# Storing all partitions of the attention's output bank, and adding its two parts where the branches load them

## The chip, the cores and the metric

One core of a Trainium2 chip runs the whole kernel. The metric is the device time of one execution in microseconds (us), as the median of several runs. The engines are TensorE (PE, with its weight loads PEld), VectorE (DVE), ScalarE (ACT), GpSimd (POOL) and SyncE (SP), which issues nearly all DMAs.

## The reference

One layer of an encoder on x of 1 x 1024 x 1024, all in float32 (`bias`, `window` and `sink` stand for longer code):

```python
h = rms_norm(x, norm_mix)
q_a, k_a, v_a, q_b, k_b, v_b, g_a, g_b = split(h @ w_in)      # 8 heads of 64; q_b 8 heads, k_b/v_b 2
o_a = softmax(q_a k_a / 8 + bias_a, window of 8 x 16 on the 16 x 64 token grid) v_a
o_b = softmax(q_b k_b / 8 + bias_b, sink, blocks within +-128 tokens) v_b
y = sigmoid(g_a) * (o_a @ w_branch_a) + sigmoid(g_b) * (o_b @ w_branch_b)
x = x + y @ w_out
h = rms_norm(x, norm_ffn)
x = x + (silu(h @ w_gate) * (h @ w_up)) @ w_down               # hidden width 2816
```

q and k are normalised per head as well.

## The kernel before

**Arithmetic.** TensorE multiplies reduced float32 (fp32r). A float32 operand is therefore split into a high part, which ACT writes by a copy, and a low part, which DVE writes by a subtract (`split`, L48 to L55; the two show up as L50 and L51). A product of two such operands takes three matmuls: high by high, high by low, low by high.

**Order of the work.** The instructions of PE stand in the order of the program. Those of DVE, ACT, POOL and SP are ordered by a scheduler, save where `tc.issue_after(x)` says that an instruction may only stand after x on its engine. A DMA on SP waits until the one issued eight before it is done.

**Attention (60 to 405 us in the trace).** The heads come in six groups, na0, sw0, na1, sw1, na2 and na3: groups of two neighbourhood heads and of four sliding-window heads, 16 heads in all. For each head and query block PE makes scores (L592, L593), and DVE, ACT and POOL turn them into probabilities `E` (L598 to L606). `flip` transposes them on PE (L616) and splits them into `ph` and `pl` (ACT, then DVE). `values` multiplies both by the values (L654). The stationary operand of that product holds the high part of v in columns 0 to 63 and the low part in columns 64 to 127, so the bank `o` collects the products with the high part in partitions 0 to 63 and those with the low part in 64 to 127. A head has two halves of 512 tokens, and there is one bank `o` (L39): the next half's first product waits until `store_half` has emptied it. Between the steps of the heads PE works through a list of other products: the projections of later groups, and the first gates (`pg`, L427 to L429).

**Emptying the bank.** `store_half` (L624 to L640) copies the half of the partitions that is not the head's own into the tile `of` (ACT, L636, 64 x 512) and adds the head's own half to it (DVE, L637, 64 x 512). Two heads of a pair fill 64 partitions each of one `of`, and after the second a DMA of 512 KB takes it to `o_dram` (L640), eight in all. `of` has one buffer.

**Gates.** Eight pairs of gates, d = 0 to 7. Those of d = 0 and 1 are plain products in the attention (their results `graw`, L454, go to `g_dram`); from d = 2 on `gate_pair` computes two by two blocks by seven products instead of eight (class `Seven`), p = 1 to 7, into four banks X, Y, V and Z. After some products a bank is copied to another by ACT (L836) to go on accumulating, and DVE reads the banks into `go` (L882 to L901). Gates 2 and 3 run product by product in turn and are marked `early`; their second operands, the row sums `ta`, `tb`, `hs` (L502 to L515), are made by DVE and ACT meanwhile, those of j = 0 and 1 still in the attention, each step of them after the instruction that `att["bound"]` names (L478): the last row maximum (L598). The weights of a gate come as `ga` and `gb`.

**Branches.** A row r of `o` is 128 features by 1024 tokens: rows 0 to 3 the neighbourhood heads, 4 to 7 the sliding-window heads. `load_o` (L924 to L928) loads four rows of one half, 256 KB each, and splits each. It is called four times: rows 4 to 7, half 0, after gate 5; rows 0 to 3, half 0, behind p = 6 of gate 7; rows 4 to 7, half 1, behind p = 2; rows 0 to 3, half 1, behind p = 3, with the two loads of the first sigmoid inputs (`load_sg(0, 0)`) ahead of it. Then 16 turns follow, each with two sigmoids on ACT (L993) and two products of twelve matmuls, first over rows 4 to 7, then over rows 0 to 3 (`pb`, L427 to L429); the second half is first used in the third turn.

Output projection and feed-forward follow, by the same seven products.

Of the kernel before, what the change touches and what calls it, by code (L numbers as in the profile page):

```python
# [19 lines left out]
HD = 64  # L20
# [5 lines left out]
def block_kernel(ctx, tc, x, xt, small, w_in, rpb, t5, w_ba, w_bb, w_out, w_gate, w_up, w_down,  # L26
# [18 lines left out]
    def f(ap):  # L45
        return ap.bitcast(F32)
# [40 lines left out]
    def half_cols(h):  # L87
        return slice(h * 512, h * 512 + 512)
# [6 lines left out]
    def dma(dst, src):  # L95

        tc.keep_in_program_order(nc.sync.dma_start(dst, src))
# [4 lines left out]
    def tok(t):  # L102
        return slice(t * P, (t + 1) * P)
# [68 lines left out]
    load_small()  # L172
    load_x(0, 0, 0)

    o_dram = drp.tile([8 * P, T], F32, name="o_dram")
    swe = drp.tile([8, 512], F32, name="swe")
    nae = drp.tile([64, 744], F32, name="nae")
    g_dram = drp.tile([32 * P, 512], F32, name="g_dram")
# [253 lines left out]
    def run(gen):  # L432
        for _ in gen:
            pass
# [94 lines left out]
    with tc.tile_pool(name="at", bufs=1) as ap:  # L529
# [48 lines left out]
        for gi, (kind, idx) in enumerate(order):  # L578
            nq, nk = (2, 2) if kind == "na" else (4, 1)
            heads += [dict(gi=gi, kind=kind, hl=hl, kl=hl * nk // nq, h=idx * nq + hl, nq=nq, O={}, E={}, P={})  # L580
                      for hl in range(nq)]
        of_tiles = {}

        def scores(hd, qb):
            q, k1, k2, v = groups[hd["gi"]]
# [23 lines left out]
        def flip(hd, kb):  # L609
            q0, q1 = max(0, kb - 1), min(7, kb + 1)  # L610
            n = (q1 - q0 + 1) * P
            nm_ = f"{hd['gi']}_{hd['hl']}_{kb}"
            tp = bank("t", "tp" + nm_)
            for j, qq in enumerate(range(q0, q1 + 1)):
                ko = (kb - max(0, qq - 1)) * P
                nc.tensor.transpose(tp[:, tok(j)], hd["E"][qq][:, ko:ko + P], ident)  # L616
            ph = ap.tile([P, 384], F32R, tag="ph", name="ph" + nm_, bufs=4)
            pl = ap.tile([P, 384], F32R, tag="pl", name="pl" + nm_, bufs=4)
            split(*(z[:, :n].rearrange("p (j i) -> p j i", i=P) for z in (ph, pl)),
                  tp[:, :n].rearrange("p (j i) -> p j i", i=P)[:, :, ::-1])  # L620
            hd["P"][kb] = (ph, pl)

        def store_half(hd, half):
            gi, e = hd["gi"], hd["hl"] % 2  # L624
            pair = (gi, hd["hl"] // 2)
            if pair not in of_tiles:
                of_tiles[pair] = ap.tile([P, T], F32, tag="of", name=f"of{gi}_{hd['hl']}", bufs=1)
            of = of_tiles[pair]
            own, oth = slice(e * HD, e * HD + HD), slice(HD - e * HD, 2 * HD - e * HD)
            O = hd["O"][half]  # L630
            if hd["kind"] == "na":
                dst, sh = of[own, half_cols(half)], lambda z: z
            else:
                dst = of[own, :].rearrange("p (s r c) -> p r s c", r=16, s=8)[:, 8 * half:8 * half + 8]
                sh = lambda z: z.rearrange("p (r s c) -> p r s c", r=8, s=8)
            nc.scalar.copy(dst, sh(O[oth, :]))  # L636
            nc.vector.tensor_add(dst, sh(O[own, :]), dst)  # L637
            if e == 1 and half == 1:
                row = ((0 if hd["kind"] == "na" else 4) + hd["h"] // 2) * P
                nc.sync.dma_start(o_dram[row:row + P, :], of)  # L640

        def values(hd, block):

# [152 lines left out]
    class Seven:  # L796
# [27 lines left out]
        def step(self, p, rows=None):  # L824

            hi, lo = self.prepare(p)
            z = {1: "X", 2: "X", 5: "V", 6: "Z" if self.early else "Y", 3: "Y"}.get(p, "Z")
            ps = self.banks[z]
            for j in range(self.n) if rows is None else rows:
                bh, bl = self.mv[p][j]  # L830
                first, end = j == 0 and (p in (1, 5) or self.early and p == 3), j == self.n - 1
                nc.tensor.matmul(ps, hi[:, tok(j)], bh, start=first, stop=False, skip_group_check=True)  # L832
                nc.tensor.matmul(ps, hi[:, tok(j)], bl, start=False, stop=False, skip_group_check=True)  # L833
                nc.tensor.matmul(ps, lo[:, tok(j)], bh, start=False, stop=end, skip_group_check=True)  # L834
            if p == 1 or p == 6 and not self.early:
                nc.scalar.copy(self.banks["Z" if self.early or p == 6 else "Y"], ps)  # L836

    class TokenSums(dict):

# [84 lines left out]
    def load_o(r0, half):  # L924
        for r in range(r0, r0 + 4):
            o_rows[r, half] = hi, lo = operand("H", f"o{r}_{half}")
            dma(f(lo), o_dram[tok(r), half_cols(half)])
            split(hi, lo, f(lo))  # L928


    wb, sgs = {}, {}
# [31 lines left out]
        load_branch(1)  # L963
        load_o(4, 1)

    def behind_three():
        load_sg(0, 0)
        load_o(0, 1)

    run(gate_pair(7, ORDER, {6: lambda: load_o(0, 0), 2: behind_two, 3: behind_three}))  # L970

    sets = bank_sets()
    my = {}
# [2 lines left out]
    def out_loads(i):  # L976
# [3 lines left out]
                w_out[0, :, tok(2 * i + a)].rearrange("(k p) c -> p k c", p=P))  # L980
        return Seven(f"o{i}", [two(z) for z in st], 4, my, sets)

    turns = [(2 * j + e, half) for j in range(4) for half in range(2) for e in range(2)]
    y = {}
    for n, (d, half) in enumerate(turns):
        j, c = d // 2, half_cols(half)
        if half == 0:
            y[d] = scratch2(f"y{d}")
        if n + 1 < len(turns):
            load_sg(*turns[n + 1])  # L990
        for br in (1, 0):
            sg = sgs[d, half, br]
            nc.scalar.activation(sg, sg, AF.Sigmoid)  # L993
        for br in (1, 0):
            pb = bank(RING[(2 * n + 1 - br) % 8], f"pb{d}_{br}_{half}")
            sg = sgs[d, half, br]
            run(product(pb, wb[d, br], [o_rows[4 * br + r, half] for r in range(4)]))
            if br:
                nc.vector.tensor_mul(y[d][:, c], pb, sg)
            else:  # L1000
                nc.vector.tensor_mul(sg, pb, sg)
                nc.vector.tensor_add(y[d][:, c], y[d][:, c], sg)
        if half == 0:
            p = 2 if d % 2 else 1
            my[p][j] = operand("U" if p == 1 else "V", f"y{p}_{j}")
            split(*my[p][j], y[d][:, c])
            if j < 3:
                load_branch(d + 2)
            elif d == 7:
                my[7], my[3] = ([operand("H", f"y{p}_{i}") for i in range(4)] for p in (7, 3))  # L1010
                for m, q in enumerate((7, 3)):
                    for i in range(3):
                        hi, lo = my[q][i]
                        row = (3 * m + i) * P
                        dma(f(lo), y_dram[row:row + P, :])
                        split(hi, lo, f(lo))
        elif d % 2:
            (b11, b12), (b21, b22) = halves(y[d - 1]), halves(y[d])
            t = TokenSums(f"y{j}", b11, b12, b22).rest(b21)
            for p in (5, 6):  # L1020
                my[p][j] = operand("U" if p == 5 else "V", f"y{p}_{j}")
                split(*my[p][j], t[p][0])
            for m, p in enumerate((7, 3, 4)):
                row = (3 * m + j) * P
                if j < 3:
                    dma(y_dram[row:row + P, :], t[p][0])
        if n == len(turns) - 2:
            pairs = {i: out_loads(i) for i in range(2)}
# [490 lines left out]
```

## Time and profile before

| | |
|---|---|
| median of 3 runs | 1326.53 us (1325.66 to 1327.61) |
| the profiled execution | 1324.66 us, its span 1322.9 us |
| PE busy in the span | 1306.8 us (99%) |
| DVE, ACT | 1037.3 us (78%), 699.3 us (53%) |
| granted clock of PE | 1.00 |

The profile shows one execution. A row of the timeline gives start, duration, engine, line and operation, what is written and read, the shape, and in brackets how long the engine stood idle before it and what released it. Rows of waits give the total, the number and the longest. Rows by stretch give the busy time of PE, PEld, DVE, ACT and POOL with the number of instructions, then PE's granted clock, the share of the DMA engines and GB/s. The buffers of a tile share a name in the trace: `o<-o_dram` are the loads of all rows.

### The profile page before, as it was taken

What the parts mean: (1) busy time and instruction counts of PE and PEld (TensorE: products, weight loads), DVE (VectorE), ACT (ScalarE), POOL (GpSimd) and SP (SyncE); (2) the same over time, 40 slices, a digit from 0 to 9 for tenths busy, and PEclk for the clock granted to TensorE, in tenths of its full rate; (3) what the DMA queues carried; (4) which work ended last, traced back from release to release, by engine and by line L of the source; (5) the groups of instructions that cost most, each with busy time, mean ns of one, the idle gap of its engine ahead of it and who ended that gap; (6) DMA issues with size and microseconds to landing.
All of it is one profiled execution on the core that took longest, in us unless ns stands there. A gap on an engine that the chain in (4) does not pass through costs nothing.

```text
span 1322.9 us, 19555 instructions
## 1 busy us (share of the span) xinstructions
PE 1306.8 (99%) x6618; PEld 1133.3 (86%) x6618; DVE 1037.3 (78%) x2069; ACT 699.3 (53%) x1459; POOL 172.4 (13%) x308
## 2 busy tenths in 40 slices
PE   9999999999999999999999999999999999999998
PEld 8999999999878788888887888888888888888887
DVE  5678878887787756778899887887777789798764
ACT  6667857786663334536457544434444456363532
POOL 1364645454220000000000000000000000000000
PEclk9999999999999999999999999999999999999999
DMA  9531313141424345748684532333333346672532
GB/s 311 145 88 40 92 51 94 45 118 51 130 88 167 116 138 166 250 145 259 203 290 120 159 112 80 98 118 100 92 112 119 121 167 215 239 255 64 178 129 83
DMA packets 177284, 183.52 MB, mean 139 GB/s; under 512 B 20464, under 2 KB 125936, under 8 KB 177184
## 3 DMA queue, kind: packets, MB, share of 16 engines
q1 hardware_dynamic: 176928, 182.18, 43.8%
q8 instruction: 52, 0.85, 0.3%
q14 instruction: 48, 0.39, 0.1%
q10 hardware_dynamic: 256, 0.10, 0.0%
HBM read 129.00 MB, written 48.18 MB: 134 GB/s over the span
## 4 chain that ended last, share of the span: by engine, by line
PE 84%; DVE 6%; DMA 4%; ACT 3%; issue 2%; POOL 1%; SPq 0%; ACTq 0%; DVEq 0%; POOLq 0%
PE bankZ L832 5%; PE bankZ L833 5%; PE bankZ L834 5%; PE bankY L833 5%; PE bankY L832 5%; PE bankY L834 5%; PE bankX L832 4%; PE bankX L834 4%; PE bankX L833 4%; PE pj L327 4%; PE pj L325 4%; PE pj L326 4%; PE bankV L833 3%; PE bankV L832 3%; PE bankV L834 3%; PE o L654 3%
## 5 line engine op out<-in xcount | busy, mean ns | idle before, releaser
L604 ACT ACTIVATE E<-E,nm 128x384 f32<-128x384 f32 (+3 forms) x128 | 75.7, 591 | 48.7 <-DVE nm L598 42.9
L606 POOL TENSOR_SCALAR E<-E,nm 128x384 f32<-128x384 f32 (+1 forms) x128 | 78.9, 617 | 103.8 <-DVE nm L605 72.3
L51 DVE TENSOR_TENSOR pl<-tp,ph 128x384 fp32r<-128x384 f32 (+1 forms) x128 | 66.3, 518 | 10.6 <-ACT ph L50 9.4
L50 ACT CAST ph<-tp 128x384 fp32r<-128x384 f32 (+1 forms) x128 | 57.4, 448 | 20.7 <-PE tp L616 19.6
L50 ACT CAST f<-f 128x512 fp32r<-128x512 f32 x87 | 51.3, 619 | 27.4 <-DMA f<-u_dram 22.4
L51 DVE TENSOR_TENSOR f<-f 128x512 fp32r<-128x512 f32 x87 | 56.5, 686 | 8.8 <-ACT f L50 8.7
L616 PE MATMUL tp<-ident,E 128*128 128x128 f32 x352 | 59.6, 273 | 0.1
L654 PE MATMUL o<-pl,v 128*128 128x256 f32 (+2 forms) x160 | 49.2, 308 | 4.0 <-DVE pl L51 3.9
L616 PEld LDWEIGHTS tp<-ident,E 128*128 128x128 f32 x352 | 45.2, 140 | 5.2 <-POOL E L606 0.3
L345 POOL TENSOR_TENSOR ss<-ss,mhalf 128x4 f32<-128x4 f32 (+2 forms) x42 | 49.1, 1170 | 3.1
L654 PE MATMUL o<-ph,v 128*128 128x256 f32 (+2 forms) x160 | 46.2, 303 | 3.2 <-DVE of L637 3.2
L592 PE MATMUL s<-k,q 128*128 128x384 f32 (+1 forms) x128 | 46.4, 363 | 0.0
L1213 POOL TENSOR_TENSOR rs<-rs,mhalf 128x4 f32<-128x4 f32 x2 | 2.9, 1444 | 321.5 <-DVE rs L1212 321.5
L593 PE MATMUL s<-k,q 128*128 128x384 f32 (+1 forms) x128 | 41.3, 323 | 0.0
L598 DVE CUSTOM_DVE_ANT_0 E<-s,bsw,cols 128x384 f32<-128x384 f32 (+1 forms) x64 | 36.8, 576 | 2.7 <-PE s L593 2.0
L1230 ACT ACTIVATE u<-u 128x512 f32<-128x512 f32 x44 | 27.7, 630 | 19.8 <-DVE u L1229 19.8
L598 DVE CUSTOM_DVE_ANT_0 E<-s,bna 128x384 f32<-128x384 f32 (+1 forms) x64 | 33.1, 517 | 4.8 <-PE s L593 4.2
L605 DVE RECIPROCAL nm<-nm 128x1 f32<-128x1 f32 x128 | 20.2, 159 | 21.1 <-ACT E L604 19.7
L1231 DVE TENSOR_TENSOR u<-u,wide_rs 128x512 f32<-128x512 f32 x44 | 30.2, 689 | 7.4 <-ACT u L1230 6.6
L654 PEld LDWEIGHTS o<-pl,v 128*128 128x128 f32 x160 | 30.1, 188 | 6.8 <-DVE pl L51 6.1
L833 PE MATMUL bankV<-f,f_5h 128*128 128x512 f32 x88 | 34.5, 392 | 1.0 <-DVE f L54 1.0
L654 PEld LDWEIGHTS o<-ph,v 128*128 128x128 f32 x160 | 30.1, 188 | 6.1 <-DVE of L637 5.3
(1266 smaller groups left out, 4650.7 us busy)
## 6 DMA issues: line engine op xcount, KB each, us to landing
f<-u_dram SPq DMA_DIRECT2D x77, 256.0 KB
wg_s<-in_w_gate_dram SPq DMA_DIRECT2D x22, 512.0 KB
u_dram<-u SPq DMA_DIRECT2D x33, 256.0 KB
sg<-g_dram SPq DMA_DIRECT2D x32, 256.0 KB
g_dram<-go SPq DMA_DIRECT2D x24, 256.0 KB
u_dram<-tau SPq DMA_DIRECT2D x22, 256.0 KB
u_dram<-tbu SPq DMA_DIRECT2D x22, 256.0 KB
rows<-in_x_dram SPq DMA_DIRECT2D x8, 512.0 KB
```

Source lines behind the costliest of these rows:

```text
L50: a = nc.scalar.copy(hi, src)
L51: b = (eng or nc.vector).tensor_tensor(lo, src, f(hi), ALU.subtract)
L325: nc.tensor.matmul(ps[:, :384], lh, his[k][:, :384], start=(k == 0), stop=False)
L326: nc.tensor.matmul(ps[:, :384], lh, los[k][:, :384], start=False, stop=False)
L598: att["bound"] = nc.vector.tensor_tensor_reduce(E[:, :n], s[:, :n], hd["bias"](qb), -1.0, sk if sw else 1e30, ALU.add, ALU.min, nm[:, 0:1] ...
L604: nc.scalar.activation(E[:, :m], E[:, :m], AF.Exp, bias=nm[:, 0:1], scale=-1.0, accum_out=nm[:, 1:2])
L606: nc.gpsimd.tensor_scalar(E[:, :n], E[:, :n], nm[:, 1:2], 1.0, op0=ALU.mult, op1=ALU.mult)
L616: nc.tensor.transpose(tp[:, tok(j)], hd["E"][qq][:, ko:ko + P], ident)
L654: nc.tensor.matmul(hd["O"][half][:, (a - half * 4) * P:(z + 1 - half * 4) * P], v[:, kb].rearrange("p a e -> p (a e)"), pp[:, (a - q0) * P ...
L832: nc.tensor.matmul(ps, hi[:, tok(j)], bh, start=first, stop=False, skip_group_check=True)
L833: nc.tensor.matmul(ps, hi[:, tok(j)], bl, start=False, stop=False, skip_group_check=True)
L834: nc.tensor.matmul(ps, lo[:, tok(j)], bh, start=False, stop=end, skip_group_check=True)
```

## The change

The copy out of the bank now takes all 128 partitions, and the add leaves the attention. `of` belongs to one head and still has one buffer; each head is stored by a DMA of its own, 16 of 512 KB, into an `o_dram` of twice the size. `load_o` loads two tiles per row, the products with the high parts (of two heads) and those with the low parts, 256 KB each, into the buffers where the split's results will stand, adds them on DVE into a scratch tile `os` of two buffers, and splits that. So 32 adds of 64 x 512 go, 16 adds of 128 x 512 come, and 16 loads and 8 stores more.

With it go three edits of the order: `att["bound"]` is also set by the subtract that writes `pl`; `load_sg(0, 0)` is called behind p = 1 of gate 7, with the branches' sigmoids held back until the copy of that gate's p = 6 (`last_copy`); and `Seven.step` keeps that copy.

```diff
-    o_dram = drp.tile([8 * P, T], F32, name="o_dram")
+    o_dram = drp.tile([16 * P, T], F32, name="o_dram")
...
-            split(*(z[:, :n].rearrange("p (j i) -> p j i", i=P) for z in (ph, pl)),
-                  tp[:, :n].rearrange("p (j i) -> p j i", i=P)[:, :, ::-1])
+            _, att["bound"] = split(*(z[:, :n].rearrange("p (j i) -> p j i", i=P) for z in (ph, pl)),
+                                    tp[:, :n].rearrange("p (j i) -> p j i", i=P)[:, :, ::-1])
...
         def store_half(hd, half):
-            gi, e = hd["gi"], hd["hl"] % 2
-            pair = (gi, hd["hl"] // 2)
-            if pair not in of_tiles:
-                of_tiles[pair] = ap.tile([P, T], F32, tag="of", name=f"of{gi}_{hd['hl']}", bufs=1)
-            of = of_tiles[pair]
-            own, oth = slice(e * HD, e * HD + HD), slice(HD - e * HD, 2 * HD - e * HD)
-            O = hd["O"][half]
+            if not half:
+                hd["of"] = ap.tile([P, T], F32, tag="of", name=f"of{hd['gi']}_{hd['hl']}", bufs=1)
+            of, O = hd["of"], hd["O"][half]
             if hd["kind"] == "na":
-                dst, sh = of[own, half_cols(half)], lambda z: z
+                nc.scalar.copy(of[:, half_cols(half)], O)
             else:
-                dst = of[own, :].rearrange("p (s r c) -> p r s c", r=16, s=8)[:, 8 * half:8 * half + 8]
-                sh = lambda z: z.rearrange("p (r s c) -> p r s c", r=8, s=8)
-            nc.scalar.copy(dst, sh(O[oth, :]))
-            nc.vector.tensor_add(dst, sh(O[own, :]), dst)
-            if e == 1 and half == 1:
-                row = ((0 if hd["kind"] == "na" else 4) + hd["h"] // 2) * P
-                nc.sync.dma_start(o_dram[row:row + P, :], of)
+                nc.scalar.copy(of.rearrange("p (s r c) -> p r s c", r=16, s=8)[:, 8 * half:8 * half + 8],
+                               O.rearrange("p (r s c) -> p r s c", r=8, s=8))
+            if half:
+                nc.sync.dma_start(o_dram[tok((0 if hd["kind"] == "na" else 8) + hd["h"]), :], of)
...
-                nc.scalar.copy(self.banks["Z" if self.early or p == 6 else "Y"], ps)
+                self.copied = nc.scalar.copy(self.banks["Z" if self.early or p == 6 else "Y"], ps).ins
...
     def load_o(r0, half):
         for r in range(r0, r0 + 4):
             o_rows[r, half] = hi, lo = operand("H", f"o{r}_{half}")
-            dma(f(lo), o_dram[tok(r), half_cols(half)])
-            split(hi, lo, f(lo))
+            for z, row in ((hi, 0), (lo, HD)):
+                src = o_dram[2 * r * P + row:2 * r * P + row + 1, half_cols(half)]
+                dma(f(z), bass.AP(src.tensor, src.offset, [[P * T, 2], [T, HD], [1, 512]]))
+            both = scratch(f"os{r}_{half}")
+            nc.vector.tensor_tensor(both, f(hi), f(lo), ALU.add)
+            split(hi, lo, both)
...
-    def behind_three():
-        load_sg(0, 0)
-        load_o(0, 1)
-
-    run(gate_pair(7, ORDER, {6: lambda: load_o(0, 0), 2: behind_two, 3: behind_three}))
+    run(gate_pair(7, ORDER, {1: lambda: load_sg(0, 0), 6: lambda: load_o(0, 0), 2: behind_two, 3: lambda: load_o(0, 1)}))
...
+    last_copy = pairs[7].copied
...
-            nc.scalar.activation(sg, sg, AF.Sigmoid)
+            with tc.issue_after(last_copy):
+                nc.scalar.activation(sg, sg, AF.Sigmoid)
```

The order of PE's instructions is the same in both kernels; lines below L623 have moved up by seven in the new one (L836 is L829 there). The order of three places has changed on the other engines.

On DVE at the last attention head (`pl_1_5` to `pl_1_7` are its last low halves, `of` with `o_1_0` is the head's first half), before:

```order
L515 SCALAR_TENSOR_TENSOR tb_5461<-xo_5379,cols,ta_5460 128x512
L51 TENSOR_TENSOR hs_1_5523<-tb_5461,hs_1_5523 128x512
L51 TENSOR_TENSOR hs_1_5499<-ta_5460,hs_1_5499 128x512
L51 TENSOR_TENSOR pl_1_5_5471<-tp_1_5_5466,ph_1_5_5470 128x384
L637 TENSOR_TENSOR of_0_5260<-o_1_0_5402,of_0_5260 64x512
L51 TENSOR_TENSOR hs_1_5535<-tb_5461,hs_1_5535 128x512
L51 TENSOR_TENSOR pl_1_6_5493<-tp_1_6_5488,ph_1_6_5492 128x384
```

And now:

```order
L454 TENSOR_TENSOR graw_0_0_5438<-pg_0_0_5309,wide_rs_110 128x512
L503 TENSOR_TENSOR ta_5445<-xe_5363 128x512
L51 TENSOR_TENSOR pl_1_5_5456<-tp_1_5_5451,ph_1_5_5455 128x384
L507 SCALAR_TENSOR_TENSOR ta_5445<-ta_5445,cols,g22h 128x512
L54 SCALAR_TENSOR_TENSOR hs_1_5462<-ta_5445,cols,hs_1_5462 128x512
L51 TENSOR_TENSOR pl_1_6_5478<-tp_1_6_5473,ph_1_6_5477 128x384
L511 SCALAR_TENSOR_TENSOR tb_5446<-xe_5363,cols,g22h 128x512
```

The add has gone, and the row sums of j = 1 stand behind the `pl` that stood behind them.

On DVE at the last product of gates 2 and 3 (`go_0_5707` and `go_0_5691` are gate 2's result in the two kernels, `s1g`, `s2g` and `g_5l` belong to the weights of gate 4), before:

```order
L51 TENSOR_TENSOR hs_3_5704<-tb_5689,hs_3_5704 128x512
L814 TENSOR_TENSOR s1g_5812<-gb_5809 128x512
L894 TENSOR_TENSOR go_0_5707<-bankZ_5553,gp_5709 128x512
L895 TENSOR_TENSOR go_0_5707<-bankY_5551,go_0_5707 128x512
L51 TENSOR_TENSOR g_5l<-s1g_5812,g_5h 128x512
```

And now:

```order
L51 TENSOR_TENSOR g_1l<-ga4s,g_1h 128x512
L807 TENSOR_TENSOR s1g_5796<-gb_5793 128x512
L51 TENSOR_TENSOR g_5l<-s1g_5796,g_5h 128x512
L807 TENSOR_TENSOR s2g_5797<-ga4s,s1g_5796 128x512
L887 TENSOR_TENSOR go_0_5691<-bankZ_5537,gp_5693 128x512
```

Two more rows of gate 4's weights stand ahead of the read of bank Z.

On ACT behind gate 5, where the first rows of `o` are split while gate 6 runs (with the numbers, since rows 4 to 7 read alike without them), before:

```order
L836 COPY bankY0_5551<-bankX0_5550 128x512
L50 CAST o4_0_6237<-o4_0_6237 128x512
L50 CAST o5_0_6241<-o5_0_6241 128x512
L50 CAST o6_0_6245<-o6_0_6245 128x512
L892 COPY gp6_6255<-bankV0_5552 128x512
L50 CAST o7_0_6249<-o7_0_6249 128x512
L836 COPY bankZ0_5553<-bankY0_5551 128x512
```

And now:

```order
L829 COPY bankY0_5535<-bankX0_5534 128x512
L50 CAST o4_0_6221<-os4_0_6224 128x512
L885 COPY gp6_6251<-bankV0_5536 128x512
L50 CAST o5_0_6228<-os5_0_6231 128x512
L50 CAST o6_0_6235<-os6_0_6238 128x512
L829 COPY bankZ0_5537<-bankY0_5535 128x512
L50 CAST o7_0_6242<-os7_0_6245 128x512
```

The copies of the banks stand ahead of one cast that they stood behind; the casts now read the sums `os`.

More of the change, by code (lines that the diff above doesn't have):

```diff
@@ L581, in block_kernel @@
                       for hl in range(nq)]
-        of_tiles = {}
         def scores(hd, qb):
```

## The prediction

> **What bounds the kernel now.** I read the page first, then the chain of waits by engine, then the busy time by stage, and last the timeline around the rows that the change touches. Busy times are in us, with the share of the span.
>
> ```profile
> span 1322.9 us, 19555 instructions
> PE 1306.8 (99%) x6618; PEld 1133.3 (86%) x6618; DVE 1037.3 (78%) x2069; ACT 699.3 (53%) x1459; POOL 172.4 (13%) x308
> ```
>
> TensorE sets the time, and the change leaves its instructions and their order alone. So all that can be won is time in which PE stands still, and all that can be lost is time in which it newly does. The waits of PE, and of its weight loads (PEld), are columns of total, number and longest:
>
> ```profile
> PE o L654 <- DVE pl L51: 3.9, 6, 1.0
> PE o L654 <- DVE of L637: 3.2, 6, 1.1
> PEld o L654 <- DVE pl L51: 6.1, 8, 1.2
> PEld o L654 <- DVE of L637: 5.3, 6, 1.5
> PEld bankZ L832 <- DVE go L894: 1.0, 2, 0.5
> PEld bankZ L832 <- DVE gp L898: 0.8, 2, 0.4
> ```
>
> The second row is the wait that the change aims at: the values products stand still until VectorE's add (L637) has emptied the only bank `o`. The first is the same product waiting for the low halves `pl`, which also come from VectorE. Both lie in the attention, before 405 us. Busy times of PE, PEld, DVE and ACT by stretch:
>
> ```profile
> 240.00:300.00 60.00, 58.85 (x386) 56.77 (x385) 51.94 (x162) 47.61 (x130) 33.62 (x73) 1.00 0.32 88
> 360.00:405.00 45.00, 42.51 (x228) 35.88 (x228) 35.89 (x87) 26.25 (x63) 8.71 (x13) 1.00 0.27 96
> 405.00:440.00 35.00, 34.88 (x152) 28.02 (x151) 29.07 (x47) 15.88 (x28) 0.00 (x0) 1.00 0.59 185
> 480.00:524.00 44.00, 43.97 (x195) 36.03 (x194) 25.73 (x40) 15.60 (x28) 0.00 (x0) 1.00 0.52 160
> 524.00:560.00 36.00, 36.00 (x160) 29.82 (x159) 27.21 (x43) 21.25 (x34) 0.00 (x0) 1.00 0.78 249
> ```
>
> In the attention PE loses 1.2 us of 60 and 2.5 of 45; where the loads and their adds land (480 to 560 us) it loses almost nothing. The gain must come from the first place, and only the second can take it back.
>
> **The stores.** The tile `of` shows both steps with min, median and max in ns, and one of the six waits looks like this in the timeline:
>
> ```profile
> L636 ACT COPY of<-o x32: 564/580/587, 87.8 to 397.6; 64x512 f32<-64x512 f32 x32
> L637 DVE TENSOR_TENSOR of<-o,of x32: 671/689/697, 88.4 to 400.5; 64x512 f32<-64x512 f32 x32
> 353.70 0.58 ACT L636 COPY of<-o 64x512 f32<-64x512 f32 x1
> 354.49 0.40 PE L428 MATMUL pg<-h,wg_0h 128*128 128x512 f32 x1
> 354.71 0.68 DVE L51 TENSOR_TENSOR wg_0l<-wg00s,wg_0h 128x512 fp32r<-128x512 f32 x1
> 354.72 0.40 PE L429 MATMUL pg<-h,wg_0l 128*128 128x512 f32 x1
> 355.43 0.69 DVE L637 TENSOR_TENSOR of<-o,of 64x512 f32<-64x512 f32 x1
> 356.17 0.33 PE L654 MATMUL o<-ph,v 128*128 128x128 f32 x1 [1.06 <-DVE of L637]
> ```
>
> PE issues such products every 0.23 us (354.49 to 354.72), so it was ready for the bank at 354.95, and ACT had finished at 354.28. The rest, 1.22 us, is DVE: the add stood behind another subtract and then took 0.69. With the copy alone the bank is free 0.67 us before PE asks. The loss is 0.16 more than the idle printed, because a matmul's bar outlasts its slot; over six waits that makes 3.2 + 6 x 0.16 = 4.2 us.
>
> The Trainium skill (*Trainium Kernel Development and Optimization*, the note "Reading a trace") says that matmul busy time is a bad measure, since matmuls are pipelined, and names the busy share of the weight loads instead. By its measure the six waits would be worth the 5.3 us of PEld, by PE's row 3.2; the pitch worked out above lies between, and I keep it.
>
> The copy now covers 128 partitions. A copy of that shape out of a bank has a row at 494.34 below, 0.57 us, against 0.58 for 64 partitions: no price. In five of the six waits ACT's copy had ended before PE was ready, as here; they sum to 3.1 us and go. The sixth stands in the busiest place, with a `pl` wait just before it:
>
> ```profile
> 389.83 0.33 PE L654 MATMUL o<-pl,v 128*128 128x128 f32 x1 [0.97 <-DVE pl L51]
> 390.89 0.58 ACT L636 COPY of<-o 64x512 f32<-64x512 f32 x1
> 391.56 0.54 DVE L51 TENSOR_TENSOR pl<-tp,ph 128x384 fp32r<-128x384 f32 x1
> 392.13 0.69 DVE L637 TENSOR_TENSOR of<-o,of 64x512 f32<-64x512 f32 x1
> 392.88 0.33 PE L654 MATMUL o<-ph,v 128*128 128x128 f32 x1 [0.96 <-DVE of L637]
> ```
>
> Together these cost 0.97 + 0.96 + 2 x 0.16 = 2.3 us. In the changed order `pl` stands ahead of the gate's row sums on DVE, but ACT has one more activation ahead of the copy (0.6 us), so I take 1.2 of the 2.3, between 0.6 and 2.3.
>
> Of the other five `pl` waits, 3.9 - 1.0 + 5 x 0.16 = 3.7 us, DVE's relief may take something: 32 adds of 0.69 are 22 us off an engine that is busy 51.94 of 60 us. But a `pl` also waits for the copy before it on ACT, and the freed time lies mostly elsewhere; I take 0.7, between 0 and 3.7. **Attention: 3.1 + 1.2 + 0.7 = 5.0 us less.**
>
> The stores double from 8 to 16 of 512 KB, and `of` has one buffer, so a head's first copy waits for the store of the head before. That is SP's queue, and ACT with the bank stand behind it. Rows of the last copy of one head and the first of the next:
>
> ```profile
> 132.19 0.58 ACT L636 COPY of<-o 64x512 f32<-64x512 f32 x1 [0.46 <-PE o L654]
> 141.91 0.58 ACT L636 COPY of<-o 64x512 f32<-64x512 f32 x1 [0.57 <-PE o L654]
> ```
>
> That leaves 141.91 - 132.77 = 9.1 us. A load of half the size, issued at 487.32 below, was cast 2.7 us later, and at the rate given there the other half adds 0.9: about 4 us, an estimate. No price; only if other rows on SP held the store up by over 5 us would ACT's copy, and with it the bank, wait for it.
>
> **The first gates (405 to 440 us).** The load `gb` stands behind the last store on SP.
>
> ```profile
> 408.20 0.69 DVE L814 TENSOR_TENSOR s1g<-gb 128x512 f32<-128x512 f32 x1 [4.43 <-DMA gb<-in_w_in_dram]
> 434.52 0.69 DVE L814 TENSOR_TENSOR s1g<-gb 128x512 f32<-128x512 f32 x1 [1.70 <-DMA gb<-in_w_in_dram]
> 435.13 0.68 DVE L894 TENSOR_TENSOR go<-bankZ,gp 128x512 f32<-128x512 f32 x1
> ```
>
> Now the store is released by ACT's copy, which ended at 397.6 + 0.6, and not by the add, which ended at 400.5 + 0.7 (rows of `of` above), and one store of row sums fewer stands between it and `gb`: `gb` follows 3 to 5 us earlier. The same order puts `s1g`, `g_5l` and `s2g`, 0.6 us each, ahead of the first L894, and the bank copy of the second gate behind nine rows of ACT that stood after it. The four old PEld waits, 1.8 us, mostly go if `gb` is early; the late copy brings 0.6 to 0.85 back. Net 0.3 less, between 0.8 less and 3.2 more.
>
> **The loads and adds.** Each load_o has eight loads, four adds and four splits, where it had four loads and four splits. Rows of the first, with DMA share and GB/s at the end of the last one:
>
> ```profile
> 487.32 1.82 SPq L97 DMA_DIRECT2D o<-o_dram  x4
> 490.00 0.62 ACT L50 CAST o<-o 128x512 fp32r<-128x512 f32 x1 [0.53 <-DMA o<-o_dram]
> 491.54 1.30 ACT L50 CAST o<-o 128x512 fp32r<-128x512 f32 x2 [0.92 <-DMA o<-o_dram]
> 494.34 0.57 ACT L836 COPY bankZ<-bankY 128x512 f32<-128x512 f32 x1 [0.50 <-PE bankY L834]
> 496.86 0.39 PE L832 MATMUL bankZ<-hs,g_7h 128*128 128x512 f32 x1
> 488.00:492.00 4.00, 4.00 (x19) 3.31 (x18) 0.69 (x1) 1.65 (x3) 0.00 (x0) 1.00 0.94 292
> ```
>
> At 292 GB/s a 256 KB load costs 0.9 us of the stream. The bank copy now stands behind three of the four casts, which need six loads: 487.3 + 1.5 for the start + 6 x 0.9 = 494.1, an add 0.69, a cast 0.62, the copy 0.57: it ends at 496.0, and PE asks at 496.86. So it is hidden by 0.85 us, and the 16 adds, 11 us of DVE, are hidden as well: DVE is busy 25.73 of 44. The last user is the branch that opens on rows 0 to 3 of the second half:
>
> ```profile
> 536.00 0.69 DVE L51 TENSOR_TENSOR o<-o 128x512 fp32r<-128x512 f32 x1
> 538.03 0.39 PE L427 MATMUL pb<-o,wb00h 128*128 128x512 f32 x1
> ```
>
> The last of its four subtracts ends at 536.7. Four more loads at 0.9 set it back by 3.5 us, less about 1 because the two sigmoid loads no longer stand ahead: 539.2, an estimate. PE asks for that row nine products after 538.03, at 540.1, so 0.9 us are to spare. Price 0; I add 0.3 for both, and 0 to 8 as bounds.
>
> The Trainium skill (*DMA: Bandwidth & Descriptors*, "Anatomy of one DMA" and "Bandwidth") speaks against this: about 2.0 us fixed per DMA plus its bytes at 436 KB per us, so loads should be batched to 1 MiB. By it one such load is an estimated 2.6 us, and the trace agrees for the first (2.68 from issue to cast); eight in a row would take 21 us, but here four were in flight at once.
>
> **Sum.** -5.0 - 0.3 + 0.3 = -5.0 us. The profiled execution took 1324.66 us (1.8 around its span), 1.87 below the median of 1326.53; off the median the same 5.0 gives 1321.5.
>
> **Rivals.** (1) The change doesn't do what it says: ACT is as late as DVE was, since copies wait their turn among exponentials. For it: ACT is busy 47.61 of 60. Against it: five copies had ended early. Then only the relief is left, 0.7 and the 0.6 at the sixth wait: 1325.2. Chance 0.11.
> (2) The first gates eat it: if `gb` is not earlier, the three rows ahead of L894 and the late copy cost 3.2 + 0.85 = 4.0 us: 1325.5. Against it: the store no longer waits for the add of 400.5. Chance 0.11.
> (3) Slower: the eight loads take t each, not 0.9. The stall at 496.86 is 6(t - 0.9) - 0.85 and at the branch 8(t - 0.9) - 0.9. It begins at t = 1.04, eats the gain at 1.4, and at 1.6 it is 3.4 + 4.7 = 8.1 us: +3, 1329.5. For it: the DMA share of 0.94 during the four loads, 0.78 in the branches. Against it: 292 GB/s were moved meanwhile. Chance 0.07. The skill's rule leads here if loads did not overlap, and further.
> (4) More: the `pl` waits go as well, 3.1 + 2.3 + 2 to 3.7: 1317.5 to 1319. Chance 0.13.
>
> **How the numbers follow.** The forecast itself has 0.58: 1321.5, with 1319.5 to 1323.5 as its own range. 1317.5 to 1326 takes in cases 1, 2 and 4, and leaves out most of case 3 and the unforeseen. 0.2% is 2.65 us, about what a measurement of this kernel can tell: faster is below 1323.9. That is the forecast and case 4, 0.71; cases 1 and 2 give 0.21 of same with a hundredth to the other side; case 3 0.08.
>
> **What would show it.** Right: no wait of L654 on `of` except one short one near 391 us, released by ACT; `pl` waits down to about 3 us; the stretch 360 to 405 with about 2 us less; `gb` landing by 405; the bank copy ending near 496.0; PE still at 44 of 44 and 36 of 36 from 480 to 560. Wrong: L654 waiting for ACT's copy six times (case 1), DVE's s1g after 408 with PE idle near 430 (case 2), or PE waits on `o` or `bankZ` near 497 and 538 (case 3).

## The result

| | median us | runs |
|---|---|---|
| before | 1325.66 | 1322.9 to 1327.61, 5 runs |
| changed | 1459.72 | 1458.36 to 1460.72, 5 runs |

The ratio is 1.1013 (95% interval 1.0996 to 1.103): the changed kernel is 134 us slower, where 5 us less had been forecast. The profiled execution of the changed kernel has a span of 1457.8 us, 134.9 more than before. The page gives the sum of it at once:

```profile
span 1457.8 us, 19593 instructions
PE 1325.1 (91%) x6618; PEld 1143.9 (78%) x6618; DVE 1027.0 (70%) x2053; ACT 695.7 (48%) x1459; POOL 171.0 (12%) x308
```

PE's idle time rises from 1322.9 - 1306.8 = 16.1 us to 1457.8 - 1325.1 = 132.7, by 116.6; and its busy time rises by 18.3 with the same 6618 instructions. The waits of PE say where it stood:

```profile
PE pb L428 <- DVE o L51: 65.2, 8, 10.0
PE bankZ L825 <- ACT bankZ L829: 26.8, 1, 26.8
PE bankZ L825 <- DVE gp L891: 26.1, 2, 22.3
PE o L647 <- DVE pl L51: 2.7, 5, 0.7
PE pb L427 <- ACT o L50: 2.6, 2, 2.1
```

No wait on the emptying of `o` is left. In its place stand the branch products, waiting for the splits of `o`'s rows, and the bank Z products of gates 6 and 7, behind a copy and two sums that stand, on ACT and DVE, behind the work on the same rows: 65.2 + 26.8 + 26.1 + 2.6 = 120.7 us; the other waits shrank by 4. By stretch (PE, PEld, DVE, ACT, POOL; PE's granted clock; DMA share; GB/s), over the first of these waits and the stages as in the prediction:

```profile
360.00:405.00 45.00, 43.78 (x231) 37.07 (x230) 35.71 (x83) 25.13 (x58) 6.64 (x11) 1.00 0.47 158
480.00:524.00 44.00, 17.17 (x69) 13.75 (x68) 4.75 (x7) 3.39 (x6) 0.00 (x0) 0.69 0.15 57
524.00:560.00 36.00, 23.68 (x91) 18.68 (x90) 15.34 (x24) 10.41 (x17) 0.00 (x0) 0.85 0.26 89
560.00:660.00 100.00, 28.76 (x76) 19.39 (x76) 18.22 (x29) 7.32 (x12) 0.00 (x0) 0.57 0.17 62
495.00:505.00 10.00, 0.00 (x0) 0.00 (x0) 1.39 (x2) 1.10 (x2) 0.00 (x0) 0.50 0.13 50
```

The last row is the one to stop at. Loads are under way, PE stands still, DVE and ACT run two instructions each, and yet the DMA engines are busy by 0.13, which is 2 of 16, and move 50 GB/s; before the change the same stage showed 0.94 and 292 GB/s. The timeline of it, on SP, DVE, ACT and PE:

```profile
481.64 29.24 SPq L97 DMA_DIRECT2D o<-o_dram  x8
495.40 0.69 DVE L924 TENSOR_TENSOR os<-o 128x512 f32<-128x512 f32 x1 [14.20 <-DMA o<-o_dram]
505.83 0.69 DVE L924 TENSOR_TENSOR os<-o 128x512 f32<-128x512 f32 x1 [8.37 <-DMA o<-o_dram]
516.30 0.69 DVE L924 TENSOR_TENSOR os<-o 128x512 f32<-128x512 f32 x1 [9.77 <-DMA o<-o_dram]
517.55 0.58 ACT L829 COPY bankZ<-bankY 128x512 f32<-128x512 f32 x1
518.18 0.80 PE L825 MATMUL bankZ<-hs,g_7h 128*128 128x512 f32 x1 [26.83 <-ACT bankZ L829]
```

Each sum needs two loads and follows the one before after 10.45 us: 5.2 us per load of 256 KB, not 0.9. The bank copy stands behind the third cast, as the order said, and ends at 518.1; PE had wanted it near 491.4. In gate 7 a sum on VectorE stands behind an add that waits for its loads:

```profile
572.48 0.69 DVE L924 TENSOR_TENSOR os<-o 128x512 f32<-128x512 f32 x1 [9.77 <-DMA o<-o_dram]
573.09 0.68 DVE L891 TENSOR_TENSOR gp<-bankZ,gp 128x512 f32<-128x512 f32 x1
573.83 0.80 PE L825 MATMUL bankZ<-hs,g_4h 128*128 128x512 f32 x1 [22.27 <-DVE gp L891]
```

The 18.3 us of busy time come with the waits. In the stretch from 495 the granted clock is 0.50. When PE starts again at 518.18 its products stand 0.43 us apart until 521.75, then 0.23 as before: 3.6 us at half speed. After the waits that end at 529.44 and 573.83 us it is 5.7 us, and between the waits of the branch products the granted clock stays at 0.50:

```profile
601.00:678.00 77.00, 15.84 (x31) 9.09 (x32) 17.00 (x28) 10.06 (x18) 0.00 (x0) 0.50 0.27 93
```

The Trainium skill (*TensorE: Matmul & The Clock Gate*, Part 1) says that the clock falls to half after an idle window of about 3.4 us and comes back after as much sustained work. The 3.6 us after the first wait agree with it; the 5.7 us after the other two are longer.

What the prediction had priced in the attention did come. The values products with the low halves, before and after, in the rows of tile `o` (the two times in us are the starts of the first and of the last one):

```profile
L654 PE MATMUL o<-pl,v x160: 273/283/443, 77.3 to 397.3; 128*128 128x256 f32 x64, 128*128 128x384 f32 x64, 128*128 128x128 f32 x32
```

```profile
L647 PE MATMUL o<-pl,v x160: 272/283/445, 77.9 to 392.3; 128*128 128x256 f32 x64, 128*128 128x384 f32 x64, 128*128 128x128 f32 x32
```

From first to last it takes 314.4 us instead of 320.0.

### The profile page after: what moved, and what is told of

Read it like the earlier page. It is cut to its first block, busy times and chain, and to the rows that moved or that the text cites. A ratio compares the mean times of both kernels' runs of the same rounds, so it can differ in the third digit from the quotient of the medians.

```text
span 1457.8 us, 19593 instructions
## 1 busy us (share of the span) xinstructions
PE 1325.1 (91%) x6618; PEld 1143.9 (78%) x6618; DVE 1027.0 (70%) x2053; ACT 695.7 (48%) x1459; POOL 171.0 (12%) x308
## 4 chain that ended last, share of the span: by engine, by line
PE 76%; DMA 9%; DVE 6%; SPq 4%; ACT 3%; issue 1%; POOL 0%; ACTq 0%; DVEq 0%; POOLq 0%
DMA o<-o_dram 5%; PE bankZ L825 5%; PE bankZ L827 5%; PE bankZ L826 5%; PE bankY L825 5%; PE bankY L826 5%; PE bankY L827 5%; SPq L97 4%; PE bankX L825 4%; PE bankX L826 4%; PE bankX L827 4%; PE pj L325 3%; PE pj L327 3%; PE pj L326 3%; PE bankV L825 3%; PE bankV L826 2%
## 5 line engine op out<-in xcount | busy, mean ns | idle before, releaser
L924 DVE TENSOR_TENSOR os<-o 128x512 f32<-128x512 f32 x16 | 11.1, 693 | 144.8 <-DMA o<-o_dram 144.8
L50 ACT CAST o<-os 128x512 fp32r<-128x512 f32 x16 | 9.9, 616 | 135.2 <-DVE os L924 135.2
L428 PE MATMUL pb<-o,wb10h 128*128 128x512 f32 x8 | 4.8, 606 | 37.5 <-DVE o L51 37.5
L825 PE MATMUL bankZ<-hs,g_4h 128*128 128x512 f32 x24 | 11.6, 483 | 26.1 <-DVE gp L891 26.1
```

The costliest lines, as they stand in the source:

```text
L50: a = nc.scalar.copy(hi, src)
```

## The experiments

Theory A: the 120 us are the description of the loads. Their source counts 2, 64 and 512 (two heads, 64 rows, 512 columns), and a source whose leading dimension counts 2 is moved by 2 DMA engines. Theory B: they are the amount, twice the loads and bytes, with an add ahead of each split.

### Plain rows: the same loads with a source of 128 equally spaced rows

```diff
-                nc.sync.dma_start(o_dram[tok((0 if hd["kind"] == "na" else 8) + hd["h"]), :], of)
+                g = (0 if hd["kind"] == "na" else 8) + hd["h"]
+                for part in range(2):
+                    row = g // 2 * 2 * P + part * P + g % 2 * HD
+                    nc.sync.dma_start(o_dram[row:row + HD, :], of[part * HD:part * HD + HD, :])
...
-            for z, row in ((hi, 0), (lo, HD)):
-                src = o_dram[2 * r * P + row:2 * r * P + row + 1, half_cols(half)]
-                dma(f(z), bass.AP(src.tensor, src.offset, [[P * T, 2], [T, HD], [1, 512]]))
+            for z, row in ((hi, 0), (lo, P)):
+                dma(f(z), o_dram[2 * r * P + row:2 * r * P + row + P, half_cols(half)])
```

> The changed kernel, with the rows of each value-high and each value-low product of a pair of heads laid side by side in DRAM (each head stored by two stores of 64 partitions), so that every load's source is one run of 128 equally spaced rows. Bytes, number of loads, adds and orders stay. Theory A (a source whose leading dimension counts 2 is moved by 2 of the 16 DMA engines): the DMA share during the loads goes from 0.13 to over 0.8, 50 GB/s to over 250, the waits of the branch products (65 us) and of bank Z (53 us) go, and the time is 1319 to 1324 us. Rival B (twice the loads, through a queue in which a load waits for the one eight before it, and an add ahead of each split): the loads still take over 5 us each and the time stays above 1400 us.

Measured: 1325.03 us against 1325.09, ratio 1.0004 (0.9994 to 1.0013). The 134 us are gone, with all bytes, loads and adds in place. B is wrong. The stretch of the first loads:

```profile
486.00:491.00 5.00, 5.00 (x24) 4.14 (x23) 0.45 (x2) 0.57 (x1) 0.00 (x0) 1.00 0.73 247
```

The share and the rate are a little under the 0.8 and 250 that A had named. But the time is 1 us above A's range: this version is no faster than the kernel before. Among its waits:

```profile
PE o L650 <- DVE pl L51: 3.5, 8, 0.7
PE pj L325 <- ACT h L53: 1.7, 2, 0.9
PE bankX L828 <- ACT bankZ L832: 1.7, 1, 1.7
PE tp L615 <- DVE pl L51: 1.1, 1, 1.1
PE tp L615 <- POOL E L605: 0.7, 2, 0.4
```

The two stores per head are one more row on SP, and the scheduler's order on DVE and ACT shifts by some rows for it. The waits for ACT's `h` lie in the first 13 us, ahead of any store; they are 0.4 us in the changed kernel's profile and none in that of the kernel before, and what made them longer here wasn't settled. Against the changed kernel, three waits for `pl` and two for POOL's `E` are new in the attention, and the wait at the second gate has grown from 0.5 to 1.7 us: the late bank copy of the prediction's second rival.

### Blocks of 32 rows: a leading dimension of 4

```diff
...
+                        row = (g // 2 * 8 + part * 4 + g % 2 * 2 + a) * 40
+                        nc.sync.dma_start(o_dram[row:row + 32, :], of[z:z + 32, :])
...
-                dma(f(z), bass.AP(src.tensor, src.offset, [[P * T, 2], [T, HD], [1, 512]]))
...
+                dma(f(z), bass.AP(src.tensor, src.offset, [[40 * T, 4], [T, 32], [1, 512]]))
```

> The changed kernel, with the head's output in DRAM in blocks of 32 rows set 40 rows apart (stored by four stores of 32 partitions), so that a load's source counts 4, 32 and 512 instead of 2, 64 and 512. Same bytes, same number of loads. Theory A: four DMA engines, share 0.25, about 100 GB/s, 5.2 us from one sum to the next instead of 10.45, and a time between 1340 and 1375 us. Rival B: no change, about 1460 us. If it is the gap in the rows as such that costs, also about 1460 us.

Measured: 1379.44 us, ratio 1.0409 (1.0391 to 1.0427), 4 us above the range that A gave. The casts and a stretch of the loads:

```profile
491.46 0.62 ACT L50 CAST o<-os 128x512 fp32r<-128x512 f32 x1 [7.25 <-DVE os L930]
496.68 0.62 ACT L50 CAST o<-os 128x512 fp32r<-128x512 f32 x1 [4.11 <-DVE os L930]
501.92 0.62 ACT L50 CAST o<-os 128x512 fp32r<-128x512 f32 x1 [4.63 <-DVE os L930]
```

```profile
490.00:500.00 10.00, 1.77 (x8) 1.13 (x6) 2.08 (x3) 1.72 (x3) 0.00 (x0) 0.69 0.26 101
```

5.2 us per pair instead of 10.45, 0.26 of the engines, 101 GB/s: twice the leading dimension, twice the rate. The source has gaps in both, so the gap as such does not explain the 134 us.

### The kernel before, with loads described by a leading 2

```diff
...
-            dma(f(lo), o_dram[tok(r), half_cols(half)])
+            src = o_dram[r * 144:r * 144 + 1, half_cols(half)]
+            dma(f(lo), bass.AP(src.tensor, src.offset, [[72 * T, 2], [T, HD], [1, 512]]))
```

> The kernel before, its store and add in the attention untouched, with each 128-row block in DRAM broken in two blocks of 64 rows set 72 rows apart (two stores of 64 partitions), so that its 16 loads are described as 2, 64 and 512. Only the description of the loads is that of the changed kernel: half its bytes, no adds. Theory A: share 0.13 and 50 GB/s in the loads, 5.2 us from cast to cast, and a time of 1345 to 1380 us. Rival B: about 1327 us.

Measured: 1390.16 us, ratio 1.049 (1.0472 to 1.0508): 65 us, 10 above the range of A, and with it goes only a second store per pair of heads, whose price wasn't measured here. The loads are half as many as in the changed kernel, so a row takes 5.2 us:

```profile
497.20 0.62 ACT L50 CAST o<-o 128x512 fp32r<-128x512 f32 x1 [5.92 <-DMA o<-o_dram]
502.42 0.62 ACT L50 CAST o<-o 128x512 fp32r<-128x512 f32 x1 [4.60 <-DMA o<-o_dram]
507.64 0.62 ACT L50 CAST o<-o 128x512 fp32r<-128x512 f32 x1 [4.60 <-DMA o<-o_dram]
```

```profile
500.00:510.00 10.00, 0.00 (x0) 0.00 (x0) 1.38 (x2) 1.72 (x3) 0.00 (x0) 0.59 0.13 50
```

With 2 the share is 0.13, with 4 it is 0.26. The Trainium skill has this as a rule (*DMA: Bandwidth & Descriptors*, "Why a DMA increments its semaphore by 16 and not by 1" and "Rules for kernel authors"): the number of engines is the largest up to 16 that divides the slowest dimensions of source and destination, so a leading dimension under 16 confines the transfer. For 2 and 4 that gives 2 and 4 engines; the shares here, 0.13 and 0.26 of 16, agree.

### Loads cut in two plain loads of 64 rows

```diff
-                src = o_dram[2 * r * P + row:2 * r * P + row + 1, half_cols(half)]
-                dma(f(z), bass.AP(src.tensor, src.offset, [[P * T, 2], [T, HD], [1, 512]]))
+                for e in range(2):
+                    at = (2 * r + e) * P + row
+                    dma(f(z)[e * HD:e * HD + HD, :], o_dram[at:at + HD, half_cols(half)])
```

> The changed kernel with its layout in DRAM, but each load cut in two plain loads of 64 rows and 128 KB, 64 in all instead of 32. Theory A: full share, 1320 to 1328 us, up to 4 us behind the version with plain loads of 128 rows where the doubled issues delay the casts. Rival B (number of loads): worse than the changed kernel, above 1460 us.

Measured: 1327.76 us, ratio 1.0017 (1.0009 to 1.0025). The number of loads is not what cost 134 us. What this version still loses lies at these loads (its profiled execution took 1324.98 us): with 16 issues per call, sums follow each other after 2.0 to 2.8 us, the branch products wait 3.0 + 0.4 us, and the granted clock falls to 0.73 in the stretch from 530 to 540 us.

### The change with nothing but the slow source removed

```diff
-            for z, row in ((hi, 0), (lo, HD)):
-                src = o_dram[2 * r * P + row:2 * r * P + row + 1, half_cols(half)]
-                dma(f(z), bass.AP(src.tensor, src.offset, [[P * T, 2], [T, HD], [1, 512]]))
+            for e, z in enumerate((hi, lo)):
+                dma(f(z), o_dram[tok(2 * r + e), half_cols(half)])
```

> The changed kernel with every store, add, split and the order of all engines left alone; only the rows that a load takes differ: the two tiles of a row are the 128 stored rows of one head and of the next, each one run of equally spaced rows, so that what is added are partitions of two heads (this leaves the right pairing out). This is the change with nothing but the slow source removed. Theory A (the rest of the prediction holds): the attention ends 5 us earlier than before, PE stands fully used from 480 to 560 us, and the time is 1318.5 to 1322.5 us. Rival C (the gain is given back behind the attention in any case, by the second gate's bank copy and by eight loads and four adds per call): 1324 to 1327 us.

Measured: 1319.22 us against 1324.85, ratio 0.9954 (0.9941 to 0.9968): 5.6 us less, and 5 had been forecast. The order of every engine is that of the changed kernel, and so are bytes, loads and adds; what this version leaves out is the right pairing, so that its sums mix the rows of two heads and its result isn't that of the reference. The longest waits of PE, without the one for `ident` at the start, and the gate 6 copy with its loads:

```profile
PE o L647 <- DVE pl L51: 2.7, 5, 0.7
PE tp L615 <- DVE pl L51: 1.1, 1, 1.1
PE bankZ L825 <- DVE r L1112: 0.8, 1, 0.8
PE bankV L826 <- DVE f L54: 0.8, 1, 0.8
PE bankX L825 <- ACT bankZ L829: 0.5, 1, 0.5
```

```profile
481.04 3.75 SPq L97 DMA_DIRECT2D o<-o_dram  x8
489.75 0.62 ACT L50 CAST o<-os 128x512 fp32r<-128x512 f32 x1 [0.75 <-DVE os L923]
490.28 0.58 ACT L829 COPY bankZ<-bankY 128x512 f32<-128x512 f32 x1
490.91 0.50 PE L825 MATMUL bankZ<-hs,g_7h 128*128 128x512 f32 x1 [0.16 <-ACT bankZ L829]
```

With 16 engines the copy comes 0.16 us late. Rival C is wrong: behind the attention little is given back. In the profiled executions the last values product starts 5.6 us earlier than before, and the span is 5.1 us shorter.

### Without the edit of the row sums' order

```diff
-            _, att["bound"] = split(*(z[:, :n].rearrange("p (j i) -> p j i", i=P) for z in (ph, pl)),
+            split(*(z[:, :n].rearrange("p (j i) -> p j i", i=P) for z in (ph, pl)),
```

> The kernel above with the third edit of the order undone: the row sums of the first gates may again stand right behind the last row maximum, not behind the last low half. Theory A: of the attention's gain the waits for VectorE's add stay gone (3 to 4 us), and the wait of about 1 us for a low half near 389 us is back, so 0.5 to 1.5 us above the kernel above. Rival D (the gain is that edit's and not that of the shorter emptying of the bank): 4 us above it, as before the change.

Measured: 1321.94 us, ratio 0.9979 (0.997 to 0.9988), 2.7 us above the kernel above (the right pairing is left out here too). That is between the two expectations: the wait for a low half is back, and longer than before the change.

```profile
386.90 0.33 PE L647 MATMUL o<-pl,v 128*128 128x128 f32 x1 [2.34 <-DVE pl L51]
```

### That edit alone, in the kernel before

> The kernel before with nothing but the edit that holds the first gates' row sums behind the last low half. In the changed kernel's order this edit was worth 2.7 us (1321.9 against 1319.2). If it works by itself, the wait for a low half near 389 us goes and the time is 1.5 to 3 us below the kernel before; if it needs VectorE's add out of the way, the two adds that stood behind row sums at 392 and 373 us still hold the bank, and the time is within 1 us of the kernel before.

The edit is the one above, the other way round. Measured: 1325.25 us against 1324.84, ratio 1.0007 (0.9998 to 1.0016). The wait near 389 is gone and the adds' waits have grown, 0.56 to 0.94 and 0.96 to 1.18, with a new stall at a gate:

```profile
374.44 0.33 PE L654 MATMUL o<-ph,v 128*128 128x128 f32 x1 [0.94 <-DVE of L637]
392.50 0.33 PE L654 MATMUL o<-ph,v 128*128 128x128 f32 x1 [1.18 <-DVE of L637]
438.81 0.47 PE L832 MATMUL bankZ<-hs,g_7h 128*128 128x512 f32 x1 [0.79 <-ACT g_6h L50]
```

By the medians, then, the change gains 2.9 us without this edit and 5.6 with it, and the edit alone gains nothing. But not all of the 2.7 lie in the attention. PE's order is the same in all of these kernels, so the start of one product can be compared. The values products of the version with the edit, of the one without it, and of the kernel before with the edit alone:

```profile
L647 PE MATMUL o<-pl,v x160: 272/283/445, 77.5 to 391.7; 128*128 128x256 f32 x64, 128*128 128x384 f32 x64, 128*128 128x128 f32 x32
L647 PE MATMUL o<-pl,v x160: 272/283/446, 77.7 to 393.1; 128*128 128x256 f32 x64, 128*128 128x384 f32 x64, 128*128 128x128 f32 x32
L654 PE MATMUL o<-pl,v x160: 273/283/444, 77.5 to 396.9; 128*128 128x256 f32 x64, 128*128 128x384 f32 x64, 128*128 128x128 f32 x32
```

Against 397.3 before, the change without the edit gains 4.2 us in the attention; the edit adds 1.4 to that, and gains 0.4 by itself. At the first branch product the first two versions are only 0.4 us apart (518.3 and 518.7), and at the end of these executions 1.8. So most of what the edit seems to gain arises behind that, where some rows of DVE and ACT stand in another order too; what it comes from was not settled.

### Half of the short loads issued by GpSimd

```diff
-                    dma(f(z)[e * HD:e * HD + HD, :], o_dram[at:at + HD, half_cols(half)])
+                    (dma if e else nc.gpsimd.dma_start)(f(z)[e * HD:e * HD + HD, :], o_dram[at:at + HD, half_cols(half)])
```

> The version with loads of 64 rows, half of them issued by GpSimd instead of SyncE. With the whole 16 engines per load, what was left of that version's loss should be the issuing of 16 loads in a row through one queue of eight: 2.0 to 2.7 us from sum to sum, branch products waiting 3.4 us. If so: under 2 us from sum to sum, no wait of the branches, 1319 to 1324 us. If it is the loads' small size as such (128 KB): no better than 1326 to 1328 us.

Measured: 1334.17 us, ratio 1.0067 (1.0055 to 1.008): worse than with SyncE alone. The four casts of the first call follow each other after 1.3 us, but half of that call's loads had landed long before: GpSimd issued them at the end of the attention, eight of them from 398 to 403 us, among the loads of the first gates.

```profile
398.19 2.37 POOL L923 DMA_DIRECT2D o<-o_dram  x4 [13.75 <-PE pg L429]
408.81 0.72 ACT L502 ACTIVATE g22h<-xo,cols 128x512 f32<-128x512 f32 x1 [2.85 <-DMA xo<-in_xt_dram]
```

In the version with SyncE alone, ACT ran the second of these rows at 405.32 without a wait. Here it waits for the load of `xo`, which shares the time with GpSimd's eight; the second gate's bank copy behind it comes 3.5 us later, and PE loses 3.4 us to it. The branch products still wait 5.1 us, with GpSimd's loads landing a median of 7.4 us after issue. So the run doesn't tell what issuing and what the small size of the loads cost.

### Plain rows, with the second gate's bank copy earlier

```diff
         for p in order:
+            with ExitStack() as late:
+                for other in pairs.values():
+                    if p == 5 and s.early and hasattr(other, "copied"):
+                        late.enter_context(tc.issue_after(other.copied))
+                s.prepare(p)
             s.step(p)
```

> The version with plain loads of 128 rows and two stores per head, and with the weights of the fifth products of gates 2 and 3 held behind both gates' copies of bank X to bank Z, so that the second copy stands ahead of four casts on ACT. If the 1.7 us stall of the bank X products at 417 us in that version comes from the late copy, it goes, and the time falls by 1.5 to 2 us, to 1322.5 to 1324 us; if the copy was late because of its data or of DVE, the stall stays and the time is 1325 us.

Measured: 1323.38 us against 1324.84, ratio 0.999 (0.9981 to 1.0). The 1.7 us stall at 417 us is gone; 0.6 of it is back at 433.71 us, where a bank Z product waits for DVE's read of the bank. Of the versions that compute the whole reference this is the fastest tried, 1.5 us under the kernel before, at the edge of what can be told.

### One head's rows per load, and the pairing on the core

```diff
...
-            nc.vector.tensor_tensor(both, f(hi), f(lo), ALU.add)
+            nc.gpsimd.tensor_copy(both[:HD], f(hi)[HD:])
+            nc.gpsimd.tensor_copy(both[HD:], f(lo)[:HD])
+            nc.vector.tensor_tensor(both[:HD], f(hi)[:HD], both[:HD], ALU.add)
+            nc.vector.tensor_tensor(both[HD:], f(lo)[HD:], both[HD:], ALU.add)
```

> The changed kernel with loads of one head's 128 stored rows each (one run of rows, one store per head), and the right pairing made on the core: GpSimd copies the low part of the one head and the high part of the other, 64 partitions each, to the other half of the sum's tile, and two adds of 64 partitions follow on VectorE. If GpSimd, idle behind the attention, moves 64 x 512 in under 1 us, the sums stay ahead of the branches and the time is 1319 to 1322 us; if it takes 2 us or more for each of the eight moves per call, the bank Z copy near 494 us and the branches wait for it and it is 1330 us or more.

> The same with the moves on ScalarE, which is busy 16 of 44 us there: 0.6 us each, 4.6 us more per call, in the queue with the bank copies. If they find room, 1319 to 1322 us; if the bank copies of gates 6 and 7 wait behind them, by 1 to 2 us each, 1322 to 1325 us.

Measured: 1347.67 us with GpSimd (ratio 1.0172, 1.0157 to 1.0187) and 1338.51 with ScalarE (1.0104, 1.0087 to 1.0121). Both expectations missed. The moves were as fast as supposed, 0.62 us on ACT and a median of 1.0 on GpSimd, but two of them, two adds, a cast and a subtract now make up each row, and what had been asked was whether the first call fits, not the last three, whose loads are issued from 502.6, 514.6 and 523.5 us on in ScalarE's version. There, the busy times of a stretch of the branches and a product that waits in it:

```profile
540.00:550.00 10.00, 4.47 (x7) 1.87 (x7) 8.74 (x15) 9.54 (x18) 0.00 (x0) 0.50 0.19 63
541.66 0.80 PE L427 MATMUL pb<-o,wb00h 128*128 128x512 f32 x1 [3.37 <-ACT o L50]
```

ACT is busy 9.54 of 10 us and DVE 8.74, while PE is busy 4.47 at a granted clock of 0.50.

## Why the prediction was wrong, step by step

**The step that failed** is the price of a load: "At 292 GB/s a 256 KB load costs 0.9 us of the stream". That rate was read from loads whose source is 128 equally spaced rows, and was carried over to loads whose source is written as `[[P * T, 2], [T, HD], [1, 512]]`. The diff showed the new form; the prediction counted bytes and issues and never asked over how many engines the form spreads. The measured price is 5.2 us. The kernel before with this form alone pays 65 us, and the change without it, the right pairing left out, gains 5.6.

**The slower rival** had the right place: loads of t us each, a stall at the gate 6 copy, then at the branches. With t = 5.2 its formula 6(t - 0.9) - 0.85 gives 25 us, and 26.8 were measured. But its t ended at 1.6, its chance was 0.07, and the price of the branches was too low by half: 8 x 4.3 - 0.9 = 33.5 against 65 us measured. (By the formula the branches' part begins at t = 1.01, not at 1.04.) The waits between 597 and 672 us are those for two calls in a row, rows 4 to 7 and rows 0 to 3 of the second half, and the formula had one. Gate 7's 22 us were not in it at all, nor were the 18.3 us more that the products took at half clock. The rule of batching that the prediction took from the Trainium skill speaks of a fixed cost per DMA, and the page gives that fit for DMAs issued by GpSimd, where the loads here are SyncE's; the one that decided stands on the same page (*DMA: Bandwidth & Descriptors*, "Rules for kernel authors") and was not drawn on.

**The attention** was right: 5.0 us were forecast, and the values products take 5.6 less in the changed kernel's own trace. All six waits on the add are gone. How the gain divides was forecast less well: the prediction had 3.1 for five waits, 1.2 for the sixth with the `pl` wait before it, and 0.7 for VectorE's relief. Without the order of the row sums the attention gains 4.2 us, although one `pl` wait grew from 0.97 to 2.34; the order adds 1.4, and only 0.4 without the shorter emptying. How much of the 4.2 are the six waits and how much VectorE's relief was not separated.

**The stores**, priced at nothing, cost nothing: ACT's copies into `of` waited for PE alone (9.0 us of ACT's idle time, 15 times, in the changed kernel), never for a store.

**The first gates**: `gb` came early, by more than the 3 to 5 us supposed (`s1g` ran at 399.2 us instead of 408.2), and the late bank copy cost 0.5 us, against 0.6 to 0.85 forecast.

**The loads' cover**, once the source is plain, was estimated at 0.85 us at the gate 6 copy, and was 0.16 us short; at the branches it held. The term that was too small is the start, 1.5 us, for which the prediction gave no row: with 2 x 0.9 for two loads it puts the first sum 3.3 us behind the first issue, and with the plain source it started 4.5 us behind (485.50 against 481.04).

## What to carry to other kernels

Read a changed transfer by its form as well as its bytes: what is the count of the leading dimension of source and of destination, and how many engines can share it? In a profile a DMA share that stays at a small multiple of one sixteenth while something waits for the transfer gives this away at a glance. And a rate taken from a trace holds for transfers of the same form only.

## What the runs showed that was not expected

- Eight loads behind each other, each by two engines, together moved the 50 GB/s that four behind each other moved in the kernel before with this form: they did not spread over other pairs of engines. SP itself was held, 29.24 us for eight issues.
- With each store cut in two, on a queue with room and with no copy waiting for a store, a few rows of DVE and ACT stood elsewhere and the time was 1325.0 us, where the single store gave 1319.2. In the two profiled executions 0.8 us of the difference arise in the first 13 us (not settled), 3.6 in the attention, where seven more short waits, for `pl`, `ph`, `E` and the copy into `of`, show 2.1 us of idle time, and 1.2 at the second gate's copy (1.7 against 0.5).
- Each long wait of PE costs more than itself: 116.6 us more of idle time came with 18.3 us more of busy time, from products at half clock.
